# Weight parts of the first two ConvFFN column pairs made during an earlier projection and passed through DRAM

## The chip, the cores and the metric

The kernel runs on one core of one Trainium2 chip. The metric is the device time of one execution in microseconds (us). Engines are named as in the profile: PE multiplies matrices, PEld loads its weights, DVE, ACT and POOL work element by element, and SP issues the DMAs. All of SP's DMAs are issued from one instruction stream in a fixed order.

## The reference, cut to what matters

One layer of a model over 1,024 tokens of width 1,024: a mixer (Fourier branch and gated delta branch, merged by gates, one output projection), then a ConvFFN with 2,816 columns. The change touches the weights of the ConvFFN's first product.

```python
def merge_branches(f_in, o_dn, z, gates, dn_norm, w_fourier, w_dn, w_out):
    ...
    y_f = fourier_mix(f_in) @ w_fourier
    y_d = o @ w_dn
    return (gates[:, :, 0] * y_f + gates[:, :, 1] * y_d) @ w_out

def ffn_sublayer(stream, shift, scale, gate, g_pre, g_post, w_up, conv_w, w_down, rows, cols):
    h = modulate(rms_norm(stream, g_pre), shift, scale)
    a, u = jnp.split(h @ w_up, 2, axis=-1)
    a = dwconv2d(a, conv_w, rows, cols)
    y = (jax.nn.silu(a) * u) @ w_down
    return stream + gate * rms_norm(y, g_post)
```

## The kernel before, in words

**How an fp32 product is made.** Each fp32 operand is split into a rounded part h and a rest l = x − h, and the product is three matmuls: h·h, h·l and l·h. A split is one copy (ACT, mostly) and one subtraction (DVE or POOL). Weights come as halves of 128×512 (256 KB): `halves` (line 526) loads one, `split_over` (533) splits it with ACT and DVE, `weights` (539) does two halves of a block. They go into a ring `wst` that holds four halves at this stage, one being multiplied and three ahead. `product` (542) issues the matmuls, `proj_rows` (1060) runs a weight block over the two halves of the tokens: 48 matmuls of 128×512 for a block of the delta branch.

**The stages that matter.** *Delta output projection* (lines 1402 to 1414): for each of eight blocks k, `weights(a["wd"][k])`, 48 matmuls, and per token half a gate loaded from DRAM and multiplied in by DVE (`used`). After every second k, `modulation(2 + k // 2)` (1370) reads eight blocks of `w_ada`, 512 KB each, into two buffers and accumulates them on DVE. *Fourier output projection* (1417 to 1441): the same with `wf`, and the loads and splits of `wo`. *Mixer's output projection* (`wo_group`, 1493, and `post`): after it come the root of the mean square (a `pow` on POOL in `mean_pow`, 1452), the transposes, and the ConvFFN's input as tiles `hh`.

**The start of the ConvFFN.** The up product is a Strassen scheme: 22 column pairs c, seven products m each, over halves u0, u1, a0, a1 of the pair's weights. The right sides (`RB`, lines 1476 to 1486 and 1547 to 1556) are sums or differences of `hh` tiles (`sum_b`: one DVE addition, then `side_b`: an ACT copy and a DVE subtraction); they are made once. The left sides are weights: `both(c)` (1585) loads four raw halves, `summed` adds two of them on POOL, `split_w` (1578) copies on ACT and subtracts on POOL. `chain` (1567) issues the 12 matmuls of one product. The first two pairs are interleaved product by product (line 1652), the other twenty follow one at a time. `conv` (1635) then runs 16 multiply-adds per pair on DVE in PSUM. The rings of `wq` hold eight raw halves, five h and five l.

**What sets the order.** All operations are recorded (`record`, 291) with a cost (`cost`, 247) and then placed by a list scheduler (`schedule`, 351): on each engine the operation of the highest rank among those that can start. The rank is the length of the chain behind the operation, less a term that grows with the recorded PE work. DMAs are modelled as one stream at 359 bytes/ns (line 289), issued at most `LEAD` = 3 us ahead of it. Every operation is issued from `issue` (347), so the profile gives line 349 for all; groups are told apart by engine, operation and shape. Buffers live in pools that are stacked from the left and the right of SBUF; a new pool's first use waits for the last use of what lay there.

Of the kernel before, what the change touches and what calls it, by code (L numbers as in the profile page):

```python
# [9 lines left out]
F32 = mybir.dt.float32  # L10
F32R = mybir.dt.float32r
AF = mybir.ActivationFunctionType
ALU = mybir.AluOpType
# [3 lines left out]
P = 128  # L17
# [7 lines left out]
NC_FF = DFF // P  # L25
EPS = 1e-6
AHEAD = 50
HALF = 512
# [160 lines left out]
class Program:  # L189
# [8 lines left out]
    def pool(self, name, bufs=1, space=None, side="left"):  # L198
        p = Pool(self, name, bufs, space, side)
        if space is None:  # L200
            self.events.append((True, p))
        return p

    def close(self, p):
        self.events.append((False, p))
# [282 lines left out]
def layer(prog, a, out):  # L488
# [149 lines left out]
    for q in range(4):  # L638
        n = (2, 4)[q // 2]
# [673 lines left out]
    def m_tile(p_, name, dtype=F32R):  # L1313
        return p_.tile([P, HALF], dtype, tag="m", name=name)
# [55 lines left out]
    def modulation(i):  # L1370
        acc = yt.tile([P, D], F32, tag="acc", name=f"acc_ada{i}", bufs=1)
        for k in range(KT):
            w = yt.tile([P, D], F32, tag="wa", name=f"wada2_{i}_{k}", bufs=2)
            sp.dma_start(w, a["w_ada"][k * P:(k + 1) * P, i * D:(i + 1) * D])
            if k == 0:
                ve.tensor_scalar(acc, w, s[:, k, 0:1], None, op0=ALU.mult)
            else:
                ve.scalar_tensor_tensor(acc, w, s[:, k, 0:1], acc, op0=ALU.mult, op1=ALU.add)
        for g in range(2):
            hs = slice(g * HALF, (g + 1) * HALF)  # L1380
            b = yt.tile([1, HALF], F32, tag="b", name=f"bada2_{i}{g}", bufs=2)
            sp.dma_start(b, a["b_ada"][:, i * D + g * HALF:i * D + (g + 1) * HALF])
            pt = ps("pd", [1, HALF], f"ada2_{i}{g}")
            te.matmul(pt, ones[:, 0:1], acc[:, hs], start=True, stop=True)
            ve.tensor_tensor(b, b, pt, op=ALU.add)
            if i in (2, 5):
                gp = yt.tile([1, HALF], F32, tag="gp", name=f"gp_{i}{g}", bufs=1)
                sp.dma_start(gp, a["gpost"][i // 3:i // 3 + 1, hs])
                ve.tensor_tensor(b, b, gp, op=ALU.mult)
                sp.dma_start(grow[i // 3:i // 3 + 1, hs], b)  # L1390
            else:
                pq = ps("pd", [P, 4], f"ada2t_{i}{g}")
                for j in range(4):
                    te.transpose(pq[:, j:j + 1], b[:, j * P:(j + 1) * P], ident[0:1, 0:1])
                o0 = (i - 3) * 8 + g * 4
                if i == 3:
                    ve.tensor_copy(mod2[:, o0:o0 + 4], pq)
                else:
                    ve.scalar_tensor_tensor(mod2[:, o0:o0 + 4], pq, 1.0, gpre[:, 8 + g * 4:12 + g * 4],
                                            op0=ALU.add, op1=ALU.mult)  # L1400

    mf = [[m_tile(mp[g], f"mf{k}{g}", F32) for g in range(2)] for k in range(KT)]
    for k in range(KT):
        wl = weights(a["wd"][k], f"d{k}")

        def used(g, hs, pt):
            gl = yt.tile([P, HALF], F32, tag="gl", name=f"g1l{k}{g}")
            sp.dma_start(gl, gd[1, k, :, hs])
            ve.scalar_tensor_tensor(mf[k][g], gl, 1.0, pt, op0=ALU.add, op1=ALU.mult)
        proj_rows(wl, half_rows(oz), f"d{k}", used)  # L1410
        if k % 2:
            modulation(2 + k // 2)
    close(yt)
    close(ozp)

# [152 lines left out]
    def chain(pt, w_, m, start):  # L1568
        n = 0
        for i in range(4):  # L1570
            ks = slice(i * P, (i + 1) * P)
            h_, l_ = RB[m][i]
            for x_, r_ in ((w_[0], h_), (w_[0], l_), (w_[1], h_)):
                te.matmul(pt, x_[:, ks], r_, start=start and n == 0, stop=n == 11,
                          skip_group_check=not start)
                n += 1
# [7 lines left out]

    def both(c):
        raw = {}
        for n, (key, at) in enumerate((("u0", 0), ("u1", 1), ("a0", 0), ("a1", 1))):
            raw[key] = wq.tile([P, HALF], F32, tag="r", name=f"r{key}_{c}", bufs=RAW)
            sp.dma_start(raw[key], a["wu"][c + (NC_FF if key[0] == "u" else 0)][:, at * HALF:(at + 1) * HALF])

        def summed(x_, y_, op, name):
            s_ = wq.tile([P, HALF], F32, tag="l", name=f"qs_{name}{c}", bufs=WL)
            po.tensor_tensor(s_, raw[x_], raw[y_], op=op)
            return split_w(s_, f"{name}{c}")
        A = ps(f"X{c % 2}", [P, HALF], f"qa{c}")
        B = ps(f"Y{c % 2}", [P, HALF], f"qb{c}")
        C = ps(("pp", FBANK)[c % 2], [P, HALF], f"qc{c}")
        u_ = upr.tile([P, T], F32, tag="u", name=f"u{c}", bufs=3)
        v_ = upr.tile([P, HALF], F32, tag="v", name=f"v{c}", bufs=2)
        ap_ = apad[c % 2]  # L1600
        inner = lambda g: ap_[:, 1 + 8 * g:9 + 8 * g, 1:GW + 1]
        grid = lambda t_: t_.rearrange("p (a b) -> p a b", b=GW)
        def step(m):
            if m == 2:
                chain(A, summed("u0", "u1", ALU.add, "m2"), 1, True)
                first(lambda: se.activation(v_, A, AF.Copy, scale=-1.0))
            elif m == 5:
                chain(B, summed("a0", "a1", ALU.add, "m5"), 4, True)
                first(lambda: ve.tensor_tensor(v_, v_, B, op=ALU.subtract))
            elif m == 1:  # L1610
                chain(C, summed("a0", "u1", ALU.add, "m1"), 0, True)
                first(lambda: ve.tensor_tensor(v_, v_, C, op=ALU.add))
            elif m == 4:
                chain(A, split_w(raw["u1"], f"m4{c}", True), 3, False)
                first(lambda: se.activation(u_[:, 0:HALF], A, AF.Copy))
            elif m == 3:
                chain(B, split_w(raw["a0"], f"m3{c}", True), 2, False)
                first(lambda: se.activation(inner(1), grid(B), AF.Copy))
            elif m == 7:
                chain(A, summed("a1", "u1", ALU.subtract, "m7"), 6, False)  # L1620
                ve.tensor_tensor(inner(0), grid(A), grid(v_), op=ALU.add)
            else:
                chain(B, summed("u0", "a0", ALU.subtract, "m6"), 5, False)
                ve.tensor_tensor(u_[:, HALF:T], B, v_, op=ALU.add)

        def first(f):
            prog.bonus = BON
            f()
            prog.bonus = 0.0

        def last():
            conv(c, ap_, inner, u_)
        return step, last
# [164 lines left out]
```

## Time and profile before

| | us |
|---|---|
| three runs, median | 2006.71 (2005.4 to 2008.88) |
| profiled execution | 2007.74 |
| its span, first to last instruction | 2006.0 |
| PE busy in the span | 1947.3 |
| DVE busy | 1388.3 |
| POOL busy | 565.0 |

The profiled execution's time is 1.7 us above its span, and 1.03 us above the median of the runs. The mean granted TensorE clock is 0.991 of full speed. A table by stretches tells how busy each engine is in a stage; the timeline of PE tells where it stood still and which engine ended that; the groups by shape give a duration for every kind of operation, and can be taken for one stretch alone.

### The profile page before, as it was taken

How to read it: one execution, taken by the hardware profiler on the slowest of the kernel's cores; microseconds unless marked ns; L12 is line 12 of the kernel's file. 1: busy time of each engine (PE TensorE's matmuls, PEld its weight loads, DVE VectorE, ACT ScalarE, POOL GpSimd, SP SyncE). 2: the span in 40 equal slices, each digit the busy share in tenths (PEclk: the TensorE clock that was granted, in tenths of full speed). 3: DMA queues.
4: the chain of work that ended last, by engine and by line, in shares of the span. 5: the costliest groups of instructions: out<-in, count | busy, mean ns of one | idle time of the engine just before them, and what ended most of it. 6: DMA issues, size and time to landing. Idle time of an engine off the chain costs nothing.

```text
span 2006.0 us, 31360 instructions
## 1 busy us (share of the span) xinstructions
PE 1947.3 (97%) x11470; PEld 1562.6 (78%) x11470; DVE 1388.3 (69%) x2868; ACT 829.7 (41%) x1948; POOL 565.0 (28%) x573
## 2 busy tenths in 40 slices
PE   7999999999999999999999999989999999999998
PEld 3878888787788887888777778757788888778876
DVE  5659687788678768754656483589988989873132
ACT  5575446455345355333431132444444344622121
POOL 3120121202111122011211000457788888500000
PEclk9999999999999999999999999989999999999999
DMA  7153352544345254233778561312222222543131
GB/s 304 53 193 103 101 156 69 151 142 149 87 135 155 59 168 149 67 104 103 252 254 282 182 216 45 116 44 87 87 83 85 84 75 84 196 156 122 57 126 53
DMA packets 180636, 257.51 MB, mean 128 GB/s; under 512 B 75921, under 2 KB 97522, under 8 KB 180482
## 3 DMA queue, kind: packets, MB, share of 16 engines
q1 hardware_dynamic: 180482, 255.51, 39.5%
q8 instruction: 90, 1.47, 0.3%
q14 instruction: 64, 0.52, 0.1%
HBM read 194.52 MB, written 60.94 MB: 127 GB/s over the span
## 4 chain that ended last, share of the span: by engine, by line
PE 74%; DVE 11%; DMA 5%; ACT 4%; issue 2%; POOL 1%; SPq 0%; DVEq 0%; POOLq 0%; ACTq 0%
PE p L349 74%; DVE m L349 10%; ACT m L349 4%; DMA m<-d 2%; DMA d<-m 2%; DVE p L349 2%; POOL m L349 1%; DMA m<-in_wi_dram 1%; ACT p L349 1%; DMA m<-in_wu_dram 0%; DMA m<-in_w_ada_dram 0%; SPq L349 0%; ACT L349 0%; DVEq L1787 0%; POOLq L1787 0%
## 5 line engine op out<-in xcount | busy, mean ns | idle before, releaser
L349 PE MATMUL p<-m,m 128*128 128x512 f32 (+5 forms) x11310 | 1934.3, 336 | 49.1 <-DVE m L349 17.9
L349 PEld LDWEIGHTS p<-m,m 128*128 128x128 f32 (+3 forms) x11310 | 1544.4, 172 | 429.7 <-issue 53.7
L349 DVE TENSOR_TENSOR m<-m,m 128x512 fp32r<-128x512 f32 (+27 forms) x1116 | 584.1, 539 | 242.6 <-ACT m L349 215.6
L349 ACT ACTIVATE m<-m 128x512 fp32r<-128x512 f32 (+8 forms) x669 | 430.5, 662 | 629.5 <-DMA m<-d 157.4
L349 POOL TENSOR_TENSOR m<-m,m 128x512 fp32r<-128x512 f32 (+5 forms) x338 | 449.8, 1353 | 832.4 <-DVE m L349 672.6
L349 ACT ACTIVATE m<-p 128x512 f32<-128x512 f32 (+4 forms) x510 | 220.9, 447 | 306.9 <-PE p L349 270.2
L349 DVE SCALAR_TENSOR_TENSOR m<-p,m,m 128x128 f32<-128x128 f32 (+4 forms) x488 | 204.0, 452 | 88.4 <-ACT m L349 38.5
L349 DVE SCALAR_TENSOR_TENSOR p<-m,m,p 128x512 f32<-128x512 f32 x352 | 240.1, 749 | 3.5 <-ACT p L349 1.2
L349 ACT ACTIVATE m<-p,m 128x128 f32<-128x128 f32 (+2 forms) x240 | 115.8, 495 | 183.1 <-PE p L349 181.9
L349 POOL MEMSET m<- 128x1024 f32 (+7 forms) x79 | 35.6, 458 | 388.0 <-PE p L349 247.3
L349 POOL COPY m<-m 32x256 f32<-32x256 f32 (+2 forms) x136 | 60.6, 448 | 149.6 <-DMA m<-d 112.2
L349 DVE SCALAR_TENSOR_TENSOR m<-m,m 128x512 f32<-128x512 f32 (+5 forms) x119 | 66.0, 560 | 24.7 <-ACT m L349 19.5
L349 DVE TENSOR_TENSOR m<-p,m 128x512 f32<-128x512 f32 (+4 forms) x91 | 57.6, 644 | 27.9 <-PE p L349 25.7
L349 DVE TENSOR_TENSOR m<-m,p 128x128 f32<-128x128 f32 (+3 forms) x117 | 53.6, 459 | 26.2 <-PE p L349 25.7
L349 DVE COPY m<-p 32x256 f32<-32x256 f32 (+11 forms) x116 | 41.8, 368 | 39.6 <-PE p L349 25.6
L349 DVE SCALAR_TENSOR_TENSOR m<-m,m,m 128x1024 f32<-128x1024 f32 (+2 forms) x68 | 57.9, 855 | 14.0 <-DMA m<-in_w_ada_dram 13.6
L349 ACT ACTIVATE p<-p 128x128 f32<-128x128 f32 x208 | 55.0, 265 | 25.1 <-PE p L349 23.5
L349 DVE SCALAR_TENSOR_TENSOR m<-m,p 128x512 f32<-128x512 f32 x76 | 50.7, 682 | 15.0 <-ACT m L349 7.8
L349 DVE SCALAR_TENSOR_TENSOR m<-m,m,p 128x128 f32<-128x128 f32 x128 | 43.3, 341 | 23.2 <-PE p L349 22.5
L349 DVE SCALAR_TENSOR_TENSOR m<-m 128x1 f32<-128x1 f32 (+1 forms) x25 | 5.4, 217 | 53.8 <-ACT m L349 53.8
L349 ACT ACTIVATION_READ_ACCUMULATOR p<-p 128x1 f32 x208 | 39.5, 190 | 0.0
L349 ACT ACTIVATE p<-m,m 128x512 f32<-128x512 f32 x44 | 30.2, 691 | 21.6 <-DVE m L349 21.3
(20 smaller groups left out, 165.7 us busy)
## 6 DMA issues: line engine op xcount, KB each, us to landing
m<-d SPq DMA_DIRECT2D x76, 512.0 KB
d<-m SPq DMA_DIRECT2D x138, 256.0 KB
m<-d SPq DMA_DIRECT2D x114, 256.0 KB
m<-in_wi_dram SPq DMA_DIRECT2D x106, 256.0 KB
m<-in_w_ada_dram SPq DMA_DIRECT2D x48, 512.0 KB
m<-in_wu_dram SPq DMA_DIRECT2D x88, 256.0 KB
m<-in_wn_dram SPq DMA_DIRECT2D x26, 512.0 KB
m<-d SPq DMA_DIRECT2D x44, 192.0 KB
```

The costliest lines, as they stand in the source:

```text
L349: return getattr(engine.real, method)(*[real(v) for v in args], **{k_: real(v) for k_, v in kw.items()})
```

## The change

Fourteen weight tiles of the ConvFFN (pairs 0 and 1, products 1 to 7) are made in the loop over k of the delta output projection, two per k until the plan is empty: a load of the raw half where it isn't there yet (eight loads of 256 KB in all), a sum on POOL for ten of them, the copy on ACT, the subtraction on POOL, and two stores of 256 KB to the DRAM tile `wsd`. The buffers are a pool of ten tiles, opened after `yt` and closed before it. In the ConvFFN, pairs 0 and 1 load no raw halves and make no sums and splits; `ready` loads h and l of each product from `wsd` into the rings `h` and `l` of `wq`. Pairs 2 to 21 are as before.

```diff
@@ layer(), ahead of the delta branch's output projection
+    NPRE = 2
+    wsd = dram.tile([NPRE, 7, 2, P, HALF], F32, name="wsd")
+    pre = pool("pre", bufs=3, side="right")
+    raws = {}
+    plan = [(c, m) for c in range(NPRE) for m in (2, 4, 5, 3, 1, 7, 6)]
+    parts_of = {2: ("u0", "u1", ALU.add), 5: ("a0", "a1", ALU.add), 1: ("a0", "u1", ALU.add), 4: ("u1",), 3: ("a0",),
+                7: ("a1", "u1", ALU.subtract), 6: ("u0", "a0", ALU.subtract)}
+
+    def raw_of(c, key):
+        if (c, key) not in raws:
+            raws[c, key] = r_ = pre.tile([P, HALF], F32, tag="r", name=f"pr{key}_{c}", bufs=4)
+            at = int(key[1])
+            sp.dma_start(r_, a["wu"][c + (NC_FF if key[0] == "u" else 0)][:, at * HALF:(at + 1) * HALF])
+        return raws[c, key]
+
+    def prepared(c, m):
+        src = raw_of(c, parts_of[m][0])
+        if len(parts_of[m]) > 1:
+            s_ = pre.tile([P, HALF], F32, tag="s", name=f"ps{c}{m}", bufs=2)
+            po.tensor_tensor(s_, src, raw_of(c, parts_of[m][1]), op=parts_of[m][2])
+            src = s_
+        h_ = pre.tile([P, HALF], F32R, tag="h", name=f"ph{c}{m}", bufs=2)
+        se.activation(h_, src, AF.Copy)
+        l_ = pre.tile([P, HALF], F32R, tag="l", name=f"pl{c}{m}", bufs=2)
+        po.tensor_tensor(l_, src, h_.bitcast(F32), op=ALU.subtract)
+        sp.dma_start(wsd[c, m - 1, 0], h_.bitcast(F32))
+        sp.dma_start(wsd[c, m - 1, 1], l_.bitcast(F32))
@@ its loop over k
         if k % 2:
             modulation(2 + k // 2)
+        for _ in range(2):
+            if plan:
+                prepared(*plan.pop(0))
+    close(pre)
     close(yt)
@@ ConvFFN, both(c)
-        for n, (key, at) in enumerate((("u0", 0), ("u1", 1), ("a0", 0), ("a1", 1))):
+        for n, (key, at) in enumerate((("u0", 0), ("u1", 1), ("a0", 0), ("a1", 1)) if c >= NPRE else ()):
...
         def summed(x_, y_, op, name):
+            if c < NPRE:
+                return ready(name)
             s_ = wq.tile([P, HALF], F32, tag="l", name=f"qs_{name}{c}", bufs=WL)
...
+        def ready(name):
+            hl = [wq.tile([P, HALF], F32R, tag=t_, name=f"q{t_}_{name}{c}", bufs=n) for t_, n in (("h", WH), ("l", WL))]
+            for e, t_ in enumerate(hl):
+                sp.dma_start(t_.bitcast(F32), wsd[c, int(name[1]) - 1, e])
+            return hl
+
+        def plain(key, name):
+            return ready(name) if c < NPRE else split_w(raw[key], f"{name}{c}", True)
...
-                chain(A, split_w(raw["u1"], f"m4{c}", True), 3, False)
+                chain(A, plain("u1", "m4"), 3, False)
...
-                chain(B, split_w(raw["a0"], f"m3{c}", True), 2, False)
+                chain(B, plain("a0", "m3"), 2, False)
```

By engine: PE, DVE, ACT and POOL issue the same numbers of rows; 24 additions and subtractions of POOL and 14 copies of ACT stand earlier; SP issues 898 DMAs in place of 842 (28 stores and 28 loads more, and 8 raw loads moved).

SP before, ahead of and in the first blocks of the delta projection (`in_wd` is that projection's weight, `in_w_ada` the modulation's, `d177` the Fourier branch's result, `d165` the gates):

```order
L349 DMA m205_9562<-in_wd_dram 128x512
L349 DMA m67_318<-in_wd_dram 128x512
L349 DMA m199_9408<-in_w_ada_dram 128x1024
L349 DMA d165_6581<-m184_9052 128x512
L349 DMA m208_9594<-d177_8877 128x512
L349 DMA m208_9594<-d177_8877 128x511
L349 DMA m71_331<-in_wd_dram 128x512
```

SP after, the same place (`d207` is `wsd`):

```order
L349 DMA m209_9570<-in_wd_dram 128x512
L349 DMA m67_318<-in_wd_dram 128x512
L349 DMA d207_9560<-m208_9566 128x512
L349 DMA d207_9560<-m210_9575 128x512
L349 DMA m200_9410<-in_w_ada_dram 128x1024
L349 DMA d166_6583<-m185_9054 128x512
L349 DMA m158_3946<-in_gpost_dram 1x512
L349 DMA d213_9609<-m196_9375 1x512
L349 DMA m214_9613<-d178_8879 128x512
L349 DMA m214_9613<-d178_8879 128x511
L349 DMA m198_9387<-in_w_ada_dram 128x1024
L349 DMA m71_331<-in_wd_dram 128x512
```

Between the third and the fourth load of `in_wd` (the second and third are the first two rows of this one) there now stand two stores to `wsd`, each of which waits for ACT or POOL; a third stands ahead of the second load. The load of `d178` (`d177` before) stands behind the stores.

POOL before, where the first pairs' sums and subtractions stood (`m1_62` is the constant of the `pow`, one of which is among them):

```order
L349 TENSOR_TENSOR m327_11115<-m322_11074,m321_11072 128x512
L349 TENSOR_TENSOR m329_11133<-m321_11072,m328_11127 128x512
L349 TENSOR_TENSOR m331_11145<-m320_11064,m319_11062 128x512
L349 TENSOR_TENSOR m300_10643<-m300_10643,m1_62 128x1
L349 TENSOR_TENSOR m334_11160<-m326_11107,m325_11101 128x512
L349 TENSOR_TENSOR m335_11170<-m327_11115,m330_11141 128x512
L349 TENSOR_TENSOR m337_11183<-m334_11160,m336_11173 128x512
L349 TENSOR_TENSOR m338_11195<-m325_11101,m332_11149 128x512
```

POOL after, from the last of the `pow` operations on:

```order
L349 TENSOR_TENSOR m318_10827<-m318_10827,m1_62 128x1
L349 MEMSET m374_11536 128x1188
L349 TENSOR_TENSOR m379_11561<-m341_11213,m338_11197 128x512
L349 TENSOR_TENSOR m383_11575<-m344_11232,m338_11197 128x512
L349 TENSOR_TENSOR m340_11208<-m379_11561,m337_11192 128x512
L349 TENSOR_TENSOR m335_11171<-m383_11575,m333_11159 128x512
L349 TENSOR_TENSOR m334_11169<-m338_11197,m330_11147 128x512
```

Behind the last `pow` there now stands a memset of the convolution's padded buffer, and the first sums after it are those of pair 2; the sums and subtractions of pairs 0 and 1 stand among POOL's rows 199 to 226, ahead of the first `pow` of the output projection.

SP before, at the start of the ConvFFN (`in_wu` are its raw halves, `d305` the mixer's result, stored tile by tile):

```order
L349 DMA d305_10681<-m290_10568 128x1024
L349 DMA m319_11062<-in_wu_dram 128x512
L349 DMA m320_11064<-in_wu_dram 128x512
L349 DMA m321_11072<-in_wu_dram 128x512
L349 DMA m322_11074<-in_wu_dram 128x512
L349 DMA m323_11084<-in_wu_dram 128x512
L349 DMA m324_11086<-in_wu_dram 128x512
L349 DMA d305_10681<-m292_10582 128x1024
L349 DMA m325_11101<-in_wu_dram 128x512
L349 DMA m326_11107<-in_wu_dram 128x512
```

SP after, the same place (`d316` is the mixer's result):

```order
L349 DMA d316_10766<-m300_10651 128x1024
L349 DMA m330_11147<-d207_9560 128x512
L349 DMA m331_11149<-d207_9560 128x512
L349 DMA m332_11157<-d207_9560 128x512
L349 DMA m333_11159<-d207_9560 128x512
L349 DMA m334_11169<-d207_9560 128x512
L349 DMA m335_11171<-d207_9560 128x512
L349 DMA d316_10766<-m303_10665 128x1024
L349 DMA m336_11186<-d207_9560 128x512
L349 DMA m337_11192<-d207_9560 128x512
L349 DMA m338_11197<-in_wu_dram 128x512
```

Six loads of raw halves have become six loads of parts from `wsd`, at the same place; more follow, and the raw loads of pair 2 begin among them.

## Rows read from the trace of the kernel before

**Rows 1.** The page of the kernel before: the busy time, share and instructions of PE, DVE and POOL over the whole execution, and from part 4 the shares of the chain that ended last, by engine.

```profile
PE 1947.3 (97%) x11470; PEld 1562.6 (78%) x11470; DVE 1388.3 (69%) x2868; ACT 829.7 (41%) x1948; POOL 565.0 (28%) x573
...
PE 74%; DVE 11%; DMA 5%; ACT 4%; issue 2%; POOL 1%; SPq 0%; DVEq 0%; POOLq 0%; ACTq 0%
```

**Rows 2.** Busy time by stretches of the execution: from and to (us), length, busy us (x instructions) of PE, PEld, DVE, ACT and POOL, then the granted TensorE clock (1.00 is the full one), the busy share of the DMA engines, and GB/s. 1059 to 1149 is the delta branch's output projection; the output projection of the mixer ends at 1290.6; 1290 to 1382 is the start of the ConvFFN.

```profile
1059.00:1100.00 41.00, 41.00 (x170) 30.83 (x171) 27.18 (x32) 3.80 (x6) 7.18 (x3) 1.00 0.82 275
1100.00:1150.00 50.00, 50.00 (x211) 37.72 (x210) 23.25 (x31) 5.86 (x10) 0.00 (x0) 1.00 0.54 176
1150.00:1205.00 55.00, 55.00 (x236) 42.65 (x235) 48.44 (x70) 19.61 (x28) 0.00 (x0) 1.00 0.65 222
...
1290.00:1305.00 15.00, 12.09 (x47) 8.47 (x45) 5.90 (x10) 7.48 (x18) 9.74 (x9) 0.89 0.18 72
1305.00:1318.00 13.00, 8.86 (x41) 5.59 (x41) 10.64 (x14) 10.38 (x19) 3.11 (x2) 0.98 0.00 0
1318.00:1344.00 26.00, 21.30 (x67) 15.10 (x68) 24.50 (x26) 9.80 (x17) 16.92 (x12) 0.81 0.25 81
1344.00:1362.00 18.00, 15.36 (x60) 11.67 (x58) 16.20 (x23) 6.70 (x13) 15.24 (x12) 0.90 0.11 36
1362.00:1382.00 20.00, 20.00 (x83) 16.24 (x82) 18.79 (x29) 9.63 (x17) 12.82 (x11) 0.92 0.22 72
1382.00:1440.00 58.00, 58.00 (x258) 47.93 (x256) 57.59 (x79) 25.33 (x45) 48.17 (x36) 1.00 0.31 103
...
1500.00:1760.00 260.00, 257.11 (x1129) 211.01 (x1128) 232.72 (x324) 122.22 (x196) 197.53 (x149) 1.00 0.32 110
```

**Rows 3.** The timeline of PE over the start of the ConvFFN: start and length (us) of each run of equal matmuls, their number, and in brackets the idle time ahead of it with the engine that ended it.

```profile
1292.65 10.86 PE L349 MATMUL p<-m,m 128*128 128x512 f32 x40 [2.05 <-ACT m L349]
...
1311.95 0.73 PE L349 MATMUL p<-m,m 128*128 128x512 f32 x2 [0.61 <-ACT m L349]
...
1316.74 0.49 PE L349 MATMUL p<-m,m 128*128 128x512 f32 x1 [1.89 <-ACT m L349]
1318.36 7.59 PE L349 MATMUL p<-m,m 128*128 128x512 f32 x20 [1.12 <-DVE m L349]
...
1448.54 51.76 PE L349 MATMUL p<-m,m 128*128 128x512 f32 x216 [3.70 <-DVE m L349]
```

**Rows 4.** The chain of waits that ended last between 1030 and 1500, in order of time: start and length (us), and what it was.

```profile
1058.95 192.39 PE p L349 x820
...
1276.55 5.27 DMA m<-in_wu_dram
1281.82 2.98 POOL m L349 x2
```

**Rows 5.** The timeline of POOL at the start of the ConvFFN, with columns as in rows 3.

```profile
1281.81 10.18 POOL L349 TENSOR_TENSOR m<-m,m 128x512 fp32r<-128x512 f32 x8 [1.64 <-DMA m<-in_wu_dram]
1292.38 3.04 POOL L349 TENSOR_TENSOR m<-m,m 128x1 f32<-128x1 f32 x3 [0.39 <-DVE m L349]
...
1335.06 1.09 POOL L349 MEMSET m<- 128x1188 f32 x1 [1.34 <-DVE m L349]
```

**Rows 6.** Groups by shape of the instructions between 1290 and 1362: count, busy us, mean ns of one, and the idle time ahead with its releasers.

```profile
L349 POOL TENSOR_TENSOR m<-m,m 128x512 fp32r<-128x512 f32 x17 | 25.6, 1517 | 14.0 <-ACT m L349 14.0
L349 ACT ACTIVATE m<-m 128x512 fp32r<-128x512 f32 x36 | 21.7, 640 | 30.8 <-DVE m L349 14.3 <-POOL m L349 10.4 <-issue 4.4
L349 DVE TENSOR_TENSOR m<-m,m 128x512 f32<-128x512 f32 x19 | 21.2, 1125 | 1.1 <-ACT m L349 0.6
L349 DVE TENSOR_TENSOR m<-m,m 128x512 fp32r<-128x512 f32 x20 | 18.7, 951 | 6.5 <-ACT m L349 6.5
L349 POOL TENSOR_TENSOR m<-m,m 128x512 f32<-128x512 f32 x12 | 16.6, 1382 | 8.9 <-PE p L349 8.9
...
L349 DVE TENSOR_TENSOR m<-m,p 128x512 f32<-128x512 f32 x4 | 2.7, 683 | 1.2 <-PE p L349 1.1
```

**Rows 7.** The same view of the delta branch's and the Fourier branch's output projections, 1059 to 1205.

```profile
L349 DVE SCALAR_TENSOR_TENSOR m<-m,m,m 128x1024 f32<-128x1024 f32 x20 | 27.3, 1366 | 8.3 <-DMA m<-in_w_ada_dram 8.3
L349 ACT ACTIVATE m<-m 128x512 fp32r<-128x512 f32 x36 | 22.6, 631 | 107.7 <-DVE m L349 44.5 <-DMA m<-in_wd_dram 27.2 <-PE p L349 24.6
...
L349 DVE TENSOR_TENSOR m<-m,m 128x512 fp32r<-128x512 f32 x20 | 13.8, 688 | 14.1 <-ACT m L349 13.9
...
L349 DVE TENSOR_TENSOR m<-m,m 128x512 f32<-128x512 f32 x16 | 10.8, 682 | 0.1
...
L349 POOL TENSOR_TENSOR m<-m,m 128x1024 fp32r<-128x1024 f32 x3 | 7.2, 2392 | 23.2 <-DVE m L349 23.2
```

**Rows 8.** The timeline of PE from before the delta branch's output projection to the end of the mixer's, with columns as in rows 3.

```profile
1039.62 19.16 PE L349 MATMUL p<-m,m 128*128 128x512 f32 x76
1058.95 231.42 PE L349 MATMUL p<-m,m 128*128 128x512 f32 x1004 [0.18 <-DVE m L349]
```

**Rows 9.** What the engines waited for between 1059 and 1150: us in total, times, the longest.

```profile
ACT m L349 <- DMA m<-in_wd_dram: 27.2, 5, 7.1
...
DVE m L349 <- DMA m<-in_w_ada_dram: 8.3, 9, 1.6
```

**Rows 10.** Single instructions of DVE in that projection, with columns as in rows 3: an accumulation of the modulation beside one of POOL's, and one without.

```profile
1075.59 2.99 DVE L349 SCALAR_TENSOR_TENSOR m<-m,m,m 128x1024 f32<-128x1024 f32 x1 [0.57 <-DMA m<-in_w_ada_dram]
...
1079.92 1.28 DVE L349 SCALAR_TENSOR_TENSOR m<-m,m,m 128x1024 f32<-128x1024 f32 x1
```

## The prediction

> **What bounds the kernel now.** I begin with the page: PE is busy for 97% of the span, DVE for 69%, POOL for 28%, and 74% of the chain that ended last is PE's [rows 1]. So time can be won only where PE stands still or runs its matmuls slowly, and lost wherever PE is made to wait. The table by stretches says where that is. Through the delta branch's and the Fourier branch's output projections PE is busy in every microsecond of 1059 to 1205, and again from 1382 to 1440 [rows 2]. Between 1290 and 1382, the start of the ConvFFN, it isn't: PE makes 298 matmuls there (47 + 41 + 67 + 60 + 83), and its granted clock is between 0.81 and 0.98 of full speed. At the rate of the stretch behind it, 58.00 / 258 = 0.2248 us each, they would take 67.0 us; they take 92. So 25.0 us are lost there, and no more than that can be won in this place. From 1500 to 1760 PE is busy for 257.11 of 260 us [rows 2], so what is won at the start isn't waited for again later.
>
> Who holds PE up there? The timeline of PE shows 2.05 us idle at 1292.65, ended by ACT, and then short gaps ended by ACT and DVE in turn [rows 3]. The chain of waits shows what stands behind the first: a load of a raw half of 5.27 us and two POOL instructions of 2.98 us ahead of the mean square's root [rows 4]; on POOL eight sums and subtractions, 10.18 us, stand in one piece from 1281.81 [rows 5]. Behind the other gaps stands DVE, which is busy for 24.50 of the 26 us from 1318 [rows 2]. It makes the right sides: 19 additions of 1125 ns and 20 subtractions of 951 ns [rows 6]. The same two kinds take 682 and 688 ns where POOL hardly runs [rows 7], and an operation of DVE that takes one input from PSUM costs 683 ns even beside POOL [rows 6]. So it is POOL's work on weights that makes DVE's slow, and PE waits for DVE.
>
> **What the change takes away at the start.** 24 POOL instructions (10 sums and 14 subtractions) and 14 ACT copies go from there. POOL has only a memset behind its last `pow`, and that memset ran at 1335.06, after a wait for DVE [rows 5]; the sums of pair 2 stand behind it, so that little of POOL's work is left beside the right sides.
> - The first gap and the delay of the `pow` operations: 2.05 us of the gap and some of the root's delays ahead of it, 2.8 us in my estimate, from 2.05 (the gap alone) up to 2.98 (the two POOL instructions in the chain).
> - DVE: 19 × (1.125 − 0.682) + 20 × (0.951 − 0.688) = 8.4 + 5.3 = 13.7 us. All of it lies in a stretch in which DVE is the busiest engine, so I count it whole.
> - What is late next: the gaps of 0.61 and 1.89 us ended by ACT [rows 3] are copies which a faster DVE doesn't shorten; I take 2.5 us off. ACT's 14 copies that go cost 14 × 0.640 = 9.0 us [rows 6], but ACT is busy for less than 40% from 1318 and I count nothing for them.
>
> Together −2.8 − 13.7 + 2.5 = −14. The bounds: −2 if only the first gap goes, −25 if all that is lost is won.
>
> The loads that replace the sums: 28 of 256 KB, while six of eight raw loads of the same size stood at the same place. 28 × 0.262 = 7.3 MB, against 2.1 MB, over some 60 us. At 275 GB/s, the rate of a full stretch [rows 2], that is 27 us of DMA in stretches whose share is 0 to 0.25 [rows 2]: I count it at nothing, with the mixer's x1 stores as the ones that would be late first. If that cover is gone, PE waits for the first products: the rival C below.
>
> **What the change adds to the delta projection.** 8 raw loads and 28 stores: 36 × 0.262 = 9.4 MB. In the profiled execution the DMA engines were busy for 0.82 of 1059 to 1100 at 275 GB/s, and for 0.54 of 1100 to 1150 [rows 2], so full occupation is about 275 / 0.82 = 335 GB/s, and 9.4 MB need 28 us of it. Free are 0.18 × 41 = 7.4 us up to 1100, 0.46 × 50 = 23 us up to 1150. The plan takes two products per block, and is empty after seven of eight blocks; so it has gone half way at about 1100. Its first half needs 14 us where 7.4 are free. The overflow is 6.6 us.
>
> Would PE notice? It has no slack at the start: it waited for a DVE subtraction of the first delta weights already, for 0.18 us [rows 8], and then runs without a gap [rows 4]. The loop is a ring of four halves, each of 24 matmuls; three halves ahead, at 146 us / 617 matmuls = 0.2366 us (the three stretches from 1059 to 1205 together [rows 2]), are 17 us. ACT waited five times and 27.2 us for `in_wd` [rows 9] without a gap on PE, so loads are late by several us against ACT, and the ring covers that. The new stores wait for POOL or ACT, and SP issues in order: a `wd` load queued behind one is late by that wait. I take the whole overflow, 6 us, as PE's loss: between 0 (the ring covers it) and 28 − 7.4 = 20 us (everything is pressed ahead of 1100, and the space up to 1150 comes too late).
>
> The rest of the stage's work: 14 ACT copies × 0.631 = 8.8 us, where ACT is busy for 9.7 of 91 us [rows 2, 7]: hidden, unless a copy stands ahead of a weight's copy (0.6 us). 24 POOL instructions × 1.38 to 1.52 us [rows 6] = 33 to 36 us on a POOL that does 7.2 us there [rows 2]: hidden as such. But they run beside DVE: the accumulation that takes 1.28 us alone took 2.99 us beside a POOL instruction [rows 10]. DVE's 50.4 us of 91 become at most 50.4 + 24 × 1.7 = 91 us by that worst case, at which it is the bound; by 0.3 to 0.4 us, the mean loss of the 39 instructions in rows 6, they become 59. I take the second, which is the nearer row since both engines work on 128×512 tiles there; it hides beside PE.
>
> The Trainium skill, page "SBUF — State Buffer", section "SBUF: two separate sides", says that a DVE operation with two SBUF inputs and a GpSimd operation that reads SBUF lock a shared port pair in turn, and that the later one stands still for the whole of the other. The slow instructions in rows 6 and 10 agree, and so does the unchanged one with a PSUM input. It is a rule against this change as much as for it: the collisions don't vanish, they move to the delta projection, where the accumulations and weight subtractions of DVE have two SBUF inputs.
>
> **The sum.** The profiled execution took 2007.74 us: −14 + 6 = −8 gives 1999.7. The median of the runs shown is 1.03 us lower than that execution, so the forecast is 1998.7 us.
>
> **The rivals.**
> - A, as summed: 1998.7 us, its own range 1992 to 2002. Chance 0.50.
> - B, the ring of weights covers all of the added DMA, and the start gains 14 to 18: 2006.7 − 16 = 1991 us. For it: no gap of PE from 1059 on although ACT waits for 7.1 us in a row [rows 9]. Against it: 0.18 us of slack at the first block [rows 8] and DMA engines busy for 0.82 [rows 2]. Chance 0.17.
> - C, the start gains little: DVE is faster, but PE then waits for ACT, for late parts from DRAM, or for the convolution of the first pairs, which held it for 3.70 us at 1448.54 [rows 3] and for which DVE is busy for 57.59 of 58 us from 1382 [rows 2]. A gain of 7 at the start and a loss of 6 in the delta projection: −1, 2006 us. Chance 0.13.
> - D, slower: the weights' loop of the delta projection becomes the bound. A half's load waits in SP's order behind a store, the store behind POOL's subtraction, that behind DVE's accumulation. The loop has 17 us; a load now takes 6 to 10 us to a finished part (7.1 of ACT's wait, 0.63 and 0.69 for the split [rows 7, 9]). If the stores add more than 7 to 11 us to it, each half is late by the rest. With 3.6 us per loop of 17, 91 us become 110: +19. With −14 at the start that is +5, 2012 us; it decides from an added 14 us on. For it: the stores stand directly ahead of `wd` loads. Against it: the free 23 us behind 1100. Chance 0.20.
>
> **How the numbers follow.** A measurement of this kernel can tell about 0.2%, 4 us, from no change. Faster: A but for its upper end that touches C's, and B: 0.65. Same: C and that end: 0.15. Slower: D, 0.20. The range has to leave out no more than 0.2: from 1989 (below lie B's better half and the −25 bound, 0.07) to 2011 (above lie most of D and the 20 us bound with little gain, 0.13).
>
> **What would show it.** In the profile after: PE without a gap from 1059 to 1205, or gaps ended by ACT or DVE of about 6 us in all, most before 1100; DVE's additions and subtractions for the right sides at 0.68 to 0.75 us each; 298 matmuls behind the mixer's projection in about 78 us rather than 92; the accumulations at over 1.5 us. The prediction is wrong if the delta projection takes over 12 us longer, or if the first convolution begins as late after the mixer's projection as before.

## The result and the profile after

The changed kernel took 1995.99 us (median of 4 runs, 1992.04 to 1996.58), the kernel before 2006.06 us (4 runs); the ratio is 0.9937, 95% interval 0.9918 to 0.9956. Two later groups of five runs gave 0.9928 (0.9916 to 0.994) each. So the gain is 10 us by the medians of the first four runs and 13 to 14.5 us by the three ratios, more than the 8 us forecast; the time is inside the range of 1989 to 2011 and 2.7 us below the forecast of 1998.7. The profiled execution took 1992.04 us with a span of 1990.3, the fastest of its group; two later traces of the same kernel are named where a single one can't settle a difference.

From the page, the busy times that answer to [rows 1]:

```profile
PE 1939.0 (97%) x11470; PEld 1560.6 (78%) x11470; DVE 1378.9 (69%) x2868; ACT 831.3 (42%) x1948; POOL 570.0 (29%) x573
```

The table by stretches, with the columns of [rows 2]. From 1059 to 1150 the DMA engines are nearly full, and POOL is busy for 37.9 us (19.35 + 18.51), where it had 7.2. From 1290 to 1382 PE now makes 363 matmuls (70 + 52 + 102 + 49 + 90) in place of 298; at 0.2248 us each these are 81.6 of 92 us, so 10.4 us are lost there in place of 25.0. PE's idle time in it fell from 14.4 us to 9.0 (92 less the busy time); the rest of what was lost, 10.6 us before and 1.4 now, is by this count matmuls that ran longer than 0.2248 us. From 1382 to 1500 it makes 515 in place of 495, some 4.5 us more:

```profile
1059.00:1100.00 41.00, 39.51 (x163) 29.00 (x162) 27.51 (x31) 7.44 (x12) 19.35 (x10) 1.00 0.94 314
1100.00:1150.00 50.00, 50.00 (x211) 37.71 (x210) 27.81 (x31) 9.58 (x15) 18.51 (x12) 1.00 0.91 312
...
1290.00:1305.00 15.00, 14.57 (x70) 10.93 (x68) 5.12 (x10) 7.31 (x16) 1.65 (x3) 1.00 0.63 222
1305.00:1318.00 13.00, 11.12 (x52) 8.16 (x53) 11.29 (x19) 8.51 (x15) 0.00 (x0) 1.00 0.32 111
1318.00:1344.00 26.00, 23.51 (x102) 18.71 (x102) 23.18 (x32) 11.65 (x19) 13.03 (x9) 1.00 0.21 65
1344.00:1362.00 18.00, 13.79 (x49) 10.37 (x48) 17.04 (x27) 6.00 (x11) 10.05 (x8) 0.81 0.21 73
1362.00:1382.00 20.00, 20.00 (x90) 16.57 (x89) 20.00 (x30) 9.37 (x17) 16.87 (x13) 1.00 0.34 113
1382.00:1440.00 58.00, 56.90 (x249) 46.21 (x249) 57.61 (x83) 26.80 (x48) 48.64 (x37) 1.00 0.27 89
1440.00:1500.00 60.00, 60.00 (x266) 49.69 (x265) 51.77 (x74) 26.33 (x45) 50.59 (x38) 1.00 0.26 88
```

The timeline of PE, with the columns of [rows 3]: two gaps in the delta projection, and then those of the ConvFFN's start. The 2.05 us at 1292.65 have become 0.34, the 3.70 at 1448.54 are gone, and a gap of 3.63 us stands at 1348, ended by ACT, behind pair 2's first sum and splits (the two later traces have it too, 3.62 us each):

```profile
1063.68 24.78 PE L349 MATMUL p<-m,m 128*128 128x512 f32 x103 [0.88 <-DVE m L349]
1089.07 204.36 PE L349 MATMUL p<-m,m 128*1 128x512 f32 x891 [0.61 <-DVE m L349]
1293.77 11.20 PE L349 MATMUL p<-m,m 128*128 128x512 f32 x52 [0.34 <-issue]
...
1311.18 0.73 PE L349 MATMUL p<-m,m 128*128 128x512 f32 x2 [0.44 <-ACT m L349]
...
1336.45 8.46 PE L349 MATMUL p<-m,m 128*128 128x512 f32 x36 [0.73 <-DVE m L349]
1348.53 1.22 PE L349 MATMUL p<-m,m 128*128 128x512 f32 x2 [3.63 <-ACT m L349]
```

How much of PE's idle time in the start was ended by ACT (in total, times, longest), before from 1290 to 1362 and after from 1293 to 1362:

```profile
PE p L349 <- ACT m L349: 10.9, 8, 2.6
```

```profile
PE p L349 <- ACT m L349: 4.3, 3, 3.6
```

ACT itself waited for DVE for 15.3 us in that stretch before and for 9.1 us after.

On POOL, the last `pow` is followed by 28 us of standing still up to the memset, and pair 2's sums begin behind it; before, it made 29 additions and subtractions between 1290 and 1362 [rows 6]. By the tables it was busy for 45.0 of these 72 us and is now for 24.7:

```profile
1324.66 1.09 POOL L349 MEMSET m<- 128x1188 f32 x1 [28.06 <-ACT m L349]
1327.59 8.26 POOL L349 TENSOR_TENSOR m<-m,m 128x512 f32<-128x512 f32 x5 [1.83 <-PE p L349]
```

One stretch tells more than the rest: from the end of the mixer's projection to the seventh convolution, with the same work on PE (601 and 602 matmuls) in both kernels. It took 168.4 us before and takes 149.6 now. Before:

```profile
1290.60:1459.00 168.40, 150.31 (x601) 116.80 (x602) 148.47 (x198) 76.16 (x137) 117.89 (x89) 0.92 0.22 74
```

After, same columns:

```profile
1293.40:1443.00 149.60, 139.50 (x602) 110.94 (x602) 133.66 (x195) 70.17 (x122) 92.13 (x69) 0.98 0.29 98
```

18.8 us are won here. PE's busy time fell by 10.8 us for the same matmuls, with a mean granted clock (between its two levels, 1.2 and 2.4 GHz) of 0.98 in place of 0.92, and its idle time by 8.0. The one low piece that is left in this trace, 0.81 from 1344 to 1362, lies around the gap of 3.63 us. DVE's busy time fell by 14.8. DVE's additions and subtractions with two SBUF inputs in that stretch, before (count, busy us, mean ns, then the idle time):

```profile
L349 DVE TENSOR_TENSOR m<-m,m 128x512 f32<-128x512 f32 x30 | 33.4, 1127 | 1.1 <-ACT m L349 0.6
L349 DVE TENSOR_TENSOR m<-m,m 128x512 fp32r<-128x512 f32 x20 | 18.7, 951 | 6.5 <-ACT m L349 6.5
```

And after, with one kind that reads PSUM (`p`) as the control:

```profile
L349 DVE TENSOR_TENSOR m<-m,m 128x512 f32<-128x512 f32 x30 | 26.5, 912 | 0.2
L349 DVE TENSOR_TENSOR m<-m,m 128x512 fp32r<-128x512 f32 x20 | 15.6, 820 | 7.3 <-ACT m L349 6.9
L349 DVE TENSOR_TENSOR m<-m,p 128x512 f32<-128x512 f32 x14 | 9.4, 679 | 1.1 <-PE p L349 1.1
```

In the delta projection the accumulations and the weights' subtractions became slower, as the forecast said; before, they took 1366 and 688 ns there [rows 7], and 1361 and 716 in the same window as these rows, 1050 to 1200. Of the two only the subtractions are a clear sign: in the kernel with loads only, below, they take 686 ns, but the accumulations 1503:

```profile
L349 DVE SCALAR_TENSOR_TENSOR m<-m,m,m 128x1024 f32<-128x1024 f32 x21 | 31.7, 1511 | 4.0 <-DMA m<-in_w_ada_dram 3.9
...
L349 DVE TENSOR_TENSOR m<-m,m 128x512 fp32r<-128x512 f32 x23 | 22.3, 974 | 12.2 <-ACT m L349 12.2
```

Ahead of the delta projection's gap of 0.88 us at 1063.68, ACT stood for 5.57 us, waiting for a store, directly before its copy of the weight half whose subtraction on DVE then took 1.81 us beside POOL:

```profile
1060.67 0.60 ACT L349 ACTIVATE m<-p 128x512 f32<-128x512 f32 x1 [5.57 <-DMA d<-m]
```

```profile
1061.82 1.81 DVE L349 TENSOR_TENSOR m<-m,m 128x512 fp32r<-128x512 f32 x1 [1.00 <-ACT m L349]
```

From 1059 to 1150 ACT waited 31.8 us for stores in all, and not at all before.

### The profile page after: what moved, and what is told of

The parts are those of the page before. It is cut to its first block, busy times and chain, and to the rows that moved or that the text cites. A ratio compares the mean times of both kernels' runs of the same rounds, so it can differ in the third digit from the quotient of the medians.

```text
span 1990.3 us, 31475 instructions
## 1 busy us (share of the span) xinstructions
PE 1939.0 (97%) x11470; PEld 1560.6 (78%) x11470; DVE 1378.9 (69%) x2868; ACT 831.3 (42%) x1948; POOL 570.0 (29%) x573
## 4 chain that ended last, share of the span: by engine, by line
PE 79%; DVE 8%; ACT 4%; DMA 4%; issue 2%; POOL 1%; SPq 0%; POOLq 0%; DVEq 0%; ACTq 0%
PE p L349 79%; DVE m L349 7%; ACT m L349 4%; DMA d<-m 2%; POOL m L349 1%; DVE p L349 1%; DMA m<-d 1%; ACT p L349 1%; DMA m<-in_wi_dram 0%; DMA m<-in_w_ada_dram 0%; DMA m<-in_wu_dram 0%; SPq L349 0%; ACT L349 0%; DVEq L1830 0%; POOLq L1830 0%
## 5 line engine op out<-in xcount | busy, mean ns | idle before, releaser
L349 PE MATMUL p<-m,m 128*128 128x512 f32 (+5 forms) x11310 | 1925.9, 336 | 41.8 <-DVE m L349 14.4
L349 DVE TENSOR_TENSOR m<-m,m 128x512 fp32r<-128x512 f32 (+27 forms) x1116 | 575.8, 531 | 243.1 <-ACT m L349 214.2
L349 DVE SCALAR_TENSOR_TENSOR m<-m,m 128x512 f32<-128x512 f32 (+5 forms) x119 | 66.0, 560 | 23.2 <-ACT m L349 18.1
L349 POOL TENSOR_SCALAR_AFFINE_SELECT m<-m 128x1024 f32<-128x1024 f32 x16 | 19.5, 1235 | 67.0 <-DVE m L349 67.0
```

What stands on the lines that cost most here:

```text
L349: return getattr(engine.real, method)(*[real(v) for v in args], **{k_: real(v) for k_, v in kw.items()})
```

## The experiments

In all of them "the stretch" is the one from the mixer's projection to the seventh convolution. Each is timed against the kernel before on its own chip.

**The cost alone.** The parts are made and stored, but not used:

```diff
-        for n, (key, at) in enumerate((("u0", 0), ("u1", 1), ("a0", 0), ("a1", 1)) if c >= NPRE else ()):
+        for n, (key, at) in enumerate((("u0", 0), ("u1", 1), ("a0", 0), ("a1", 1))):
-            if c < NPRE:
-                return ready(name)
...
-            return ready(name) if c < NPRE else split_w(raw[key], f"{name}{c}", True)
+            return split_w(raw[key], f"{name}{c}", True)
```

> The parts are made and stored during the delta projection as in the changed kernel, but the ConvFFN makes its own again, as in the kernel before: only the cost of the change is left. My theory, from the trace of the changed kernel (two gaps of PE of 0.88 and 0.61 us, ended by DVE, and an end of the mixer's projection some 3 us later): 1 to 3 us above the kernel before, ratio 1.0005 to 1.0015. Rival 1, the overflow of the DMA engines of my prediction: 6 us, ratio 1.003. Rival 2, the ring of weights covers all: 0 us, ratio 1.000.

Measured: 2007.88 us against 2006.99, ratio 1.0001 (0.9993 to 1.001, 11 runs): 0.2 us, −1.4 to 2.0. That is nearest to rival 2; the lower part of my theory isn't excluded, rival 1 is. The trace does show the gaps of my theory, and the mixer's projection ends 3.3 us later than before (1295.97 less the wait of 2.09 is 1293.9; before, 1290.6):

```profile
1048.65 13.04 PE L349 MATMUL p<-m,m 128*1 128x512 f32 x49 [0.54 <-DVE m L349]
1061.98 0.98 PE L349 MATMUL p<-m,m 128*128 128x512 f32 x3 [0.29 <-ACT m L349]
1063.66 24.81 PE L349 MATMUL p<-m,m 128*128 128x512 f32 x103 [0.69 <-DVE m L349]
1089.40 204.48 PE L349 MATMUL p<-m,m 128*1 128x512 f32 x891 [0.93 <-DVE m L349]
1295.97 1.43 PE L349 MATMUL p<-m,m 128*128 128x512 f32 x5 [2.09 <-ACT m L349]
```

But the stretch behind took 165.5 us in place of 168.4, with the same instructions as before and a clock of 0.96 where it had been 0.92:

```profile
1293.90:1459.40 165.50, 144.71 (x601) 112.82 (x602) 148.14 (x197) 76.12 (x137) 117.74 (x89) 0.96 0.23 76
```

PE's idle time in that stretch even grew, from 18.1 us to 20.8; what made it shorter are the same matmuls at a higher clock, 144.71 us in place of 150.31. So 3 us between two traces aren't 3 us in the runs. In the changed kernel's later two traces the mixer's projection ended at 1292.5 and 1291.7, 1.9 and 1.1 us later than in the trace of the kernel before, where its first trace has 2.8; with loads only, below, it ended at 1292.1.

**The gain alone.**

```diff
-            if plan:
+            if len(plan) > 13:
                 prepared(*plan.pop(0))
...
-                sp.dma_start(t_.bitcast(F32), wsd[c, int(name[1]) - 1, e])
+                sp.dma_start(t_.bitcast(F32), wsd[0, 1, e])
```

> Only the first product's parts are made and stored; the ConvFFN loads that one product's h and l for all 14 products, so the other 13 are left out of the computation and the output is another. All loads of the start are there, the delta projection has almost nothing added: only the gain is left. Theory: 13 to 16 us below the kernel before, ratio 0.992 to 0.9935, and 1 to 3 us below the changed kernel. Rival, that the delta projection's part is free: the same as the changed kernel, 0.995.

Measured: ratio 0.9919 (0.9906 to 0.9932), a gain of 16 us. That was on another chip than the changed kernel, so I ran both side by side later:

> The kernel with loads only, beside the changed kernel on one chip: what the making of the parts costs in the end. Theory (DVE is the bound from the right sides to the seventh convolution, and the mixer's projection, which ends 1 to 3 us earlier, isn't what it waits for): 0 to 1.5 us below the changed kernel. Rival (every us of the delta projection counts): 2.5 to 4 us below it.

> The changed kernel, as the measure of the three others on this chip: ratio to the kernel before 0.992 to 0.995.

Measured: loads only 0.9931 (0.9918 to 0.9944), the changed kernel 0.9928 (0.9916 to 0.994). The medians are 1992.55 and 1991.98 us: loads only is 0.6 us slower, each within some 2.5 us. With the first experiment's 0.2 us (−1.4 to 2.0 by its interval) the rival that every us of the delta projection counts isn't borne out, though a cost of 1 to 2 us isn't excluded.

**The parts made, but not stored.** This is the first experiment's kernel without its 28 stores. The text on record describes another ConvFFN: the one that ran makes its own parts, as in the first experiment, and is to be compared with that, not with the changed kernel.

```diff
-        sp.dma_start(wsd[c, m - 1, 0], h_.bitcast(F32))
-        sp.dma_start(wsd[c, m - 1, 1], l_.bitcast(F32))
```

> As the changed kernel without its 28 stores (the ConvFFN loads a tile that nothing wrote, so the output is another). It tells what the delta projection's cost is made of. If DMA: as the kernel with loads only, 1 to 3 us below the changed kernel, and no gap of PE between 1059 and 1150. If POOL beside DVE: as the changed kernel, with its gaps of 0.9 and 0.6 us ended by DVE still there.

Measured: ratio 1.0013 (0.9998 to 1.0028), no faster than with the stores, and PE's gaps around the delta projection's start grew to 4.55 us (with the stores 2.45), ended by DVE and ACT:

```profile
1050.29 4.92 PE L349 MATMUL p<-m,m 128*1 128x512 f32 x15 [0.96 <-DVE m L349]
1056.59 8.28 PE L349 MATMUL p<-m,m 128*128 128x512 f32 x34 [1.38 <-DVE m L349]
1066.35 0.97 PE L349 MATMUL p<-m,m 128*128 128x512 f32 x3 [1.48 <-ACT m L349]
1068.05 229.02 PE L349 MATMUL p<-m,m 128*128 128x512 f32 x994 [0.73 <-DVE m L349]
```

In this trace the DMA engines have the share that they had before [rows 2], and POOL is pressed together (18.5 us of these 41 with the stores):

```profile
1059.00:1100.00 41.00, 38.79 (x160) 28.48 (x159) 31.57 (x29) 9.52 (x16) 38.16 (x20) 1.00 0.83 275
```

So the stores aren't needed for these gaps: without them POOL's work stands closer together, DVE's weight subtractions in these 41 us take 1389 ns (1197 with the stores), and ACT waited 5.01 and 2.37 us for POOL directly ahead of PE's gap of 1.48 us. With the stores POOL's work is spread over a longer time, but ACT then waits for stores, as shown above. How much of the 1.5 to 2.5 us comes from DVE beside POOL and how much from these waits, the runs don't part.

**POOL's work put back.**

```diff
+    dum = pool("dum", bufs=1, side="right")
...
+            for i_ in range({"m3": 1, "m4": 2, "m6": 2, "m7": 2}.get(name, 3)):
+                d_ = dum.tile([P, 384], F32, tag="d", name=f"dum{name}{c}{i_}", bufs=1)
+                po.tensor_tensor(d_, hl[0].bitcast(F32)[:, 0:384], hl[1].bitcast(F32)[:, 0:384], op=ALU.subtract)
             return hl
```

> The changed kernel with 32 POOL subtractions of 128x384 added at the start of the ConvFFN, each reading a product's h and l after their loads, into a tile that nobody reads: as much POOL work beside the right sides as before (24 of 128x512), with nothing that waits for its results but POOL's own queue. Theory (POOL beside DVE): DVE's additions and subtractions go back to 0.95 to 1.1 us each, and 8 to 13 us of the gain are lost, ratio to the kernel before 0.999 to 1.002. Rival (it was the chain load, sum, copy, subtraction, product that held PE): under 3 us lost, ratio at most 0.9965.

Measured: ratio 0.9979 (0.9969 to 0.9989, 11 runs), between the two. Against the changed kernel's 0.9928 and 0.9937 that is 8 to 10 us lost of 13 to 14.5. The stretch took 161.8 us, and DVE's two kinds are back at their old length while the control isn't moved:

```profile
1292.30:1454.10 161.80, 143.36 (x601) 112.37 (x602) 147.90 (x196) 70.99 (x121) 122.31 (x96) 0.97 0.27 91
```

```profile
L349 DVE TENSOR_TENSOR m<-m,m 128x512 f32<-128x512 f32 x30 | 34.4, 1171 | 0.3
L349 DVE TENSOR_TENSOR m<-m,m 128x512 fp32r<-128x512 f32 x20 | 17.4, 903 | 6.3 <-ACT m L349 6.2
L349 DVE TENSOR_TENSOR m<-m,p 128x512 f32<-128x512 f32 x14 | 9.5, 678 | 0.0
```

DVE is busy for 147.90 us again, as before (148.47), in place of 133.66. That is the collision nearly by itself: nothing on PE, ACT or DVE waits for the added instructions' results. But the mixer's last `pow` operations now stand among them in POOL's queue: from 1284 to 1307 DVE waits 3.0 us for POOL, and 1.3 us in the same place of the changed kernel, so that some 2 us of the loss can be POOL's queue. What stays won, 4.2 us (2.2 to 6.2 by the interval), belongs to the rest: the shorter chain ahead of the first products, or the clock (0.97 here); these two the runs don't part.

**One pair only.**

```diff
-    NPRE = 2
+    NPRE = 1
```

> Only pair 0 is made during the delta projection, pair 1 as in the kernel before: 12 of the 24 POOL instructions stay at the start. Theory (each POOL instruction beside DVE costs alike): half of the gain, ratio 0.9965 to 0.9985. Rival (what counted was the chain of load, sum, copy and subtraction ahead of the first products, which are pair 0's): nearly all of the gain, at most 0.9955.

> The changed kernel once more, on the chip of the next three, so that they can be compared with it: ratio to the kernel before 0.993 to 0.9955, the start of the ConvFFN as in its first trace (first convolution 47 us behind the mixer's projection).

Measured: 0.9964 (0.9952 to 0.9976), the changed kernel beside it 0.9928 (0.9916 to 0.994). Half of the POOL work away, half of the gain: the theory's case, 0.0001 outside its range, though the interval's lower end still touches the rival's 0.9955. The chain ahead of pair 0's products was away in whole. Pair 1's stayed, so this half dose alone doesn't part a collision from a chain; the POOL work put back does.

**More than two pairs.** Sixteen products, with two of pair 2 in the eighth block, run twice; and all of three pairs, three products per block:

```diff
+    plan += [(2, 2), (2, 5)]
...
-            if c < NPRE:
+            if c < NPRE or c == NPRE and name in ("m2", "m5"):
```

```diff
-    NPRE = 2
+    NPRE = 3
...
-        for _ in range(2):
+        for _ in range(3):
```

> Pair 2's first two products are made beforehand too (16 in place of 14; the eighth block of the delta projection has room for two). In the changed kernel PE stands still for 3.63 us at 1348 behind pair 2's sums and splits, and its clock is low after it. If that gap is on the path: 2 to 6 us below the changed kernel, ratio 0.991 to 0.9935. Rival: from the first convolution on DVE is the bound, and PE's gap there costs nothing: within 1.5 us of the changed kernel.

> Sixteen products again, beside the changed kernel on one chip. From its trace (first convolution 45 us behind the mixer's projection in place of 47, the seventh no earlier): within 1.5 us of the changed kernel. From its times on the last chip: 3 to 5 us below it.

> All 21 products of pairs 0 to 2 are made beforehand, three per block of the delta projection. 7 products more are 14 stores and 4 loads of 256 KB, 4.7 MB, about 14 us of a DMA that is busy for 0.91 to 0.94 there. If the ring of weights covers them and the collisions: the start gains 4 to 8 us more, ratio 0.990 to 0.9925. If not (rival D of my prediction, the delta projection's loop becomes the bound): PE gets gaps of 5 to 15 us in all between 1059 and 1150, and the ratio is 0.995 to 1.000.

Sixteen products gave 0.9909 (0.9891 to 0.9928) at first, and 0.9927 (0.9916 to 0.9939) on a second chip, each time beside a changed kernel of 0.9928: some 4 us and nothing, so no gain that repeats. The gap at 1348 fell from 3.63 to 2.63 us, and DVE then held PE up later:

```profile
1435.96 44.34 PE L349 MATMUL p<-m,m 128*128 128x512 f32 x188 [2.42 <-DVE m L349]
```

Three pairs gave 0.9925 (0.991 to 0.9939), the changed kernel beside it 0.9928. Something of both halves of the expectation happened, and the ratio is the first one's upper end. The stretch fell to 146.0 us; but PE stood still for 5.7 us in the gaps shown, and the mixer's projection ended at 1299.2, 6.7 us later than in the changed kernel's trace on that chip. Only 2.8 us of these gaps lie between 1059 and 1150, where I had expected 5 to 15. The largest one, 2.82 us, stands ahead of 1029.71 in the projection before, ended by a copy of ACT that had waited 2.14 us for a load of that projection's weights, and the granted clock behind it was 0.71 from 1030 to 1040:

```profile
1029.71 48.33 PE L349 MATMUL p<-m,m 128*128 128x512 f32 x188 [2.82 <-ACT m L349]
1079.59 0.97 PE L349 MATMUL p<-m,m 128*128 128x512 f32 x3 [1.55 <-ACT m L349]
1081.85 217.37 PE L349 MATMUL p<-m,m 128*128 128x512 f32 x945 [1.29 <-DVE m L349]
1299.54 11.17 PE L349 MATMUL p<-m,m 128*128 128x512 f32 x52 [0.32 <-issue]
```

**DVE's work taken away behind the first convolution.**

```diff
-            ve.tensor_tensor(th_, th_, u_[:, hs], op=ALU.mult)
+            (po if c < 6 else ve).tensor_tensor(th_, th_, u_[:, hs], op=ALU.mult)
```

> The changed kernel, with the last product of the first six convolutions (12 multiplications of two SBUF tiles of 128x512) made by POOL in place of DVE. If DVE is the bound from the first to the seventh convolution (about 103 us for six, PE's 43 matmuls per pair would take less): 12 x about 1.1 us leave DVE and so do their collisions; 5 to 12 us below the changed kernel, seventh convolution that much earlier, ratio 0.987 to 0.991. If POOL becomes the bound there (it is busy for 48 of 58 us from 1382), or PE: under 2 us, or slower.

Measured: 1990.33 us, ratio 0.9922 (0.9911 to 0.9934), the changed kernel beside it 0.9928: a miss, under 2 us and not clear of noise. DVE fell from 57.61 us to 46.92 of the 58 from 1382, POOL took that over, and PE has no gap at all from 1350.66 on:

```profile
1350.66 119.69 PE L349 MATMUL p<-m,m 128*128 128x512 f32 x517 [0.57 <-POOL m L349]
```

```profile
1382.00:1440.00 58.00, 58.00 (x257) 48.06 (x256) 46.92 (x71) 27.23 (x47) 54.82 (x44) 1.00 0.27 89
```

The stretch took 149.1 us, 151.5 in the changed kernel on that chip. So DVE, though busy for 99% there, held PE up for some 2 us at most: 1.4 of these 2.4 us are the 36 matmuls ahead of the gap at 1348, 9.82 us in this trace and 11.21 in the other. Behind 1350 it is PE that bounds the changed kernel. No version that I ran beats it by more than the noise.

## Why the prediction was right

**Where the time was.** "25.0 us are lost there": by the same count 14.6 of them were won, and 14 were forecast for the start. Behind the mixer's projection, the matmuls that took 91.9 us before (293 records, up to 1382.5) take 77.7 now, where the forecast had about 78. But the terms of that sum came out otherwise:
- The first gap: 2.05 us to 0.34, so 1.7 where 2.8 stood.
- DVE: the forecast took 13.7 us, additions and subtractions at 0.682 and 0.688. They came to 0.775 (18 in the window up to 1350) and 0.820: 19 × 0.350 + 20 × 0.131 = 9.3 us. Pair 2's sums run beside the last right sides from 1327.59 on; I had written that little would be left. Nor was DVE the busiest engine in all of that stretch, as I wrote: from 1290 to 1305 it is busy for 5.90 us, POOL for 9.74.
- "What is late next": I took 2.5 us off for two gaps ended by ACT, as copies that a faster DVE doesn't shorten. The trace before has 10.9 us of such gaps, and 6.6 of them went; ACT's wait for DVE fell by 6.2 us. The gap of 1.89 us is gone, that of 0.61 is 0.44. What is late next is another, the 3.63 us behind pair 2's splits. (ACT's share isn't under 40% throughout either: it is 48% from 1362 to 1382.)
- The clock: not a term of the sum. It was inside the 25 us, and I read the whole of them as waiting: 10.6 us were slower matmuls, and 9.2 of the 14.6 won are theirs, in these two traces.
- Behind 1382 I counted nothing, and some 4.5 us came from there; the rival C had named the gap of 3.70 us at 1448.54 as what would eat the gain, and it went away instead.

The cause itself, POOL beside DVE, is shown by the work put back (8 to 10 us lost, of which some 2 may be POOL's queue, with the two kinds at 1171 and 903 ns again); the half dose fits it.

**The term that failed** is "I take the whole overflow, 6 us, as PE's loss". The DMA filled up as worked out (0.94 and 0.91), yet nothing of that is seen at the end: the cost alone measures 0.2 us (−1.4 to 2.0), and loads only take as long as the changed kernel within the noise. Its lower bound, 0 us by the ring of four weight halves, was the value to take. And the reason was at least not the whole: the gaps that PE has there, 1.5 us in the trace after, are ended by DVE beside POOL, behind a wait of ACT for a store, and they grow when the stores are left out. The Trainium skill's page "SBUF — State Buffer", section "SBUF: two separate sides", says that a DVE instruction with at most one SBUF input doesn't contend with GpSimd, outside of modes that use both port pairs. The runs agree with that, and with the rule cited in the forecast, in both stages: DVE's operations of 128x512 with one of two operands from PSUM stay at 677 to 686 ns, while those with two from SBUF became faster at the start and the subtractions slower in the delta projection.

**The rivals.** The changed kernel is rival B's case in the delta projection (nothing of the added work shows at the end), with the start that A had: 13 to 14.5 us. That the sum still came within 2.7 us is in part luck: its 14 us are right in total and not in their terms, its 6 us weren't there, and the later groups' medians of 1994.11 and 1991.98 us lie nearer to B's 1991. C's size, a gain of 7 at the start, is refuted by the gain; the gap of 3.63 us is a wait of the kind that it named. A delay such as D's came at another dose: with three products per block the mixer's projection ended 6.7 us later. Whether the stores caused that, as D has it, no run shows.

## What to carry to other kernels

Look for two engines that slow each other in the stretch that waits, not for the idle engine: what was won here came less from doing work earlier than from doing POOL's work where DVE had room, for most of it was lost again when other POOL work took its place. Before counting a full DMA against PE, see how far ahead the consumer's ring already runs; and when one trace shows a loss of 3 us, time the cost without the gain, since here eleven runs of it showed 0.2 us (−1.4 to 2.0).

## What was not expected of the hardware

The granted clock moves where nothing of the program differs. The changed kernel and the one with loads only run the same 36 matmuls behind the right sides. In two executions, side by side on one chip, they took 11.21 us (changed kernel, the first row) and 9.44 (loads only, the second), and in the changed kernel's first trace 8.46; the mean granted clock from 1318 to 1344 was 0.87, 0.93 and 1.00 in these three:

```profile
1334.71 11.21 PE L349 MATMUL p<-m,m 128*128 128x512 f32 x36 [0.63 <-DVE m L349]
```

```profile
1335.12 9.44 PE L349 MATMUL p<-m,m 128*128 128x512 f32 x36 [0.35 <-DVE m L349]
```

Between the mixer's end and the seventh convolution the mean clock was 0.92 in the trace before and 0.96 in the first experiment's, whose start is the same. PE's busy time differs by 5.6 us between these two. So some of the 10.8 us of PE's busy time may be the trace's and not the change's: what the idle gaps cost in clock, and what was chance, these runs don't part.
